# Nine elementwise steps of a gated delta rule and of a three-branch sum, issued on VectorE instead of GpSimd

## The chip, the cores and the metric

One core of a Trainium2 chip runs the whole program. It has TensorE (PE, with its weight loads as PEld), VectorE (DVE), ScalarE (ACT) and GpSimd (POOL), each with its own instruction queue that is worked off in order, and SyncE (SP), which here only issues DMAs. The engines wait for each other by semaphores. The metric is device time in microseconds: 1144.95 us, the median of three runs (1139.37, 1144.95, 1147.62).

## The reference

Two transformer blocks for 256 tokens of width 1024. The first block projects the tokens once and gives them to three branches (forgetting attention, a gated delta rule, stick-breaking attention). Their outputs are gated and summed; a memory attention and a feed-forward network follow, and then the second block. What the change touches is the decay of the delta rule and the gated sum:

```
qc, kc, vc, bc = chunks of 64 tokens of q * dk**-0.5, k, v, beta
gc    = cumsum(g within a chunk)
decay = exp(where(causal, gc[c] - gc[e], -inf))
kk    = kc @ kc.T
a_mat = where(strict, bc[c] * kk * decay, 0) + eye        # inverted further on
attn  = where(causal, (qc @ kc.T) * decay, 0)
...
mixed = g0 * (ya @ w_oa) + g1 * (yb @ w_ob) + g2 * (yc @ w_oc)
x     = x + mixed @ w_out
```

There are 4 heads of 128 and 4 chunks, so the 64x64 matrices of all heads and chunks fill a tile of 128 partitions x 512 elements (two chunks above each other, 8 pairs beside each other).

## The kernel before, in words

Nearly all time goes into products of activations with weights that stream from HBM, 512 KB at a time, in a fixed order. SP loads such a piece into one of three buffers (`raw`). ACT writes its rounded high part (`wh`, line 669), DVE the rest (`wl <- raw - wh`, line 670), and PE multiplies high by high, low by high and high by low (lines 508 to 558). A `raw` buffer is free for the next load when its `wl` is made. Up to four split pieces (`WEIGHTS = 4`) stand ready before PE.

Everything else (attention heads, the delta rule, norms, gates) is written as generators that yield where they would wait. While the program is built, a planner (`Pace` and `Stream`, lines 143 to 569) estimates when each engine is free and each operand is ready, and puts a generator's next step between the matmuls when its operands are expected. So the queues have one fixed order at run time, and it comes from the planner's costs: `70 + n / 0.96` ns for DVE, `150 + n * 2.1` ns for POOL (lines 206 to 209). Every instruction is issued through one helper, so the profile gives line 294 for all of them; they are told apart by their tiles.

The two places of the change:

- `Gdn.gates` (lines 1081 to 1150) makes the decay masks while PE is busy with the input projections. For each pair of heads (`j` = 0, 1) PE broadcasts the cumulated gates, DVE subtracts (`g<-pat,cols`), ACT makes `egB` and the exponentials `E` and `Eb`, and line 1136 multiplies `Eb` by `E`. Lines 1145 to 1148 then make `Em = E * m1l * eb`, `Eu = Eb * u1` and `E = E * uinc` of 128x512. Around them in DVE's queue are the `wl` of the weights and the convolution of the delta rule's inputs: one evacuation into `ypad`, two ACT steps and six `SCALAR_TENSOR_TENSOR g<-ypad,vec,g` of 128x256 for each pair of heads (lines 1152 to 1163).
- `mix` (lines 1729 to 1758) gates a branch's product with its output weights. The first branch writes the sum (`w_oc`), the second (`w_oa`, four pieces) multiplies and then adds into it at line 1743, the last (`w_ob`) does both on DVE.

Tiles: `g_893` holds `E` and `Eb`, `g_892` is `egB`, `g_1091` holds `Em` and `Eu`; `g_659` and `g_881` are convolved inputs; `sg` are gates, `a_280` and `a_286` the gated sum, `pmm` and `pat` tiles of PSUM.

Of the kernel before, what the change touches and what calls it, by code (L numbers as in the profile page):

```python
# [9 lines left out]
ALU = mybir.AluOpType  # L10
# [1017 lines left out]
class Gdn:  # L1028
# [52 lines left out]
    def gates(self):  # L1081

        K, nc = self.K, self.K.nc
        c, tl, v8 = self.c, self.tl, self.v8
        ident = K.C("ident")
        yield from K.room(pat=1)
        pc = K.pat()
        for t in range(2):
            nc.tensor.transpose(pc[:, t * 128:t * 128 + 68], c[0:68, t * P:t * P + P], ident[0:68, 0:68])
            nc.tensor.transpose(pc[:, 256 + t * 128:256 + t * 128 + 4], tl[64:68, t * P:t * P + P],  # L1090
                                ident[64:68, 64:68])
        K.drop(row=1)
        yield
        cols = K.p["tiny"].tile([P, 4, 4, 2], F32, tag="cols", bufs=1, name=K.nm("cols"))
        pcv = pc.rearrange("p (a t m) -> p a m t", a=2, t=2)
        lb, gc, be, tail = (cols[:, i] for i in range(4))
        nc.vector.tensor_copy(lb, pcv[:, 0, 32:36, :])
        nc.vector.tensor_copy(gc, pcv[:, 0, 64:68, :])
        nc.vector.tensor_copy(tail, pcv[:, 1, 0:4, :])
        K.drop(pat=1)  # L1100
        nc.vector.tensor_tensor(be, lb, gc, op=ALU.add)
        yield
        ecol = K.p["tiny"].tile([P, 4, 4, 2], F32, tag="ecol", bufs=1, name=K.nm("ecol"))
        nc.scalar.activation(ecol, cols, AF.Exp)
        self.eb, self.ebe, self.etail = ecol[:, 0], ecol[:, 2], ecol[:, 3]
        yield
        self.egB = K.g4()
        E, Eb = self.halves(K.g4())
        own = lambda a, c: a.rearrange("p (a m) -> p a m", a=4)[64 * c:64 * c + 64, :, 64 * c:64 * c + 64]
        for j in range(2):  # L1110
            hs, js = slice(2 * j, 2 * j + 2), slice(4 * j, 4 * j + 4)
            yield from K.room(pat=1)
            pg = K.pat()
            for h in range(2):
                K.mm(pg[:, h * T:h * T + T], K.sel("sel64", 2 * j + h), self.cg, True, True)
            yield
            for b in range(2):
                r = slice(64 * b, 64 * b + 64)
                gcb = gc[r, hs, :].rearrange("p h t -> p (h t)")[:, :, None].to_broadcast([64, 4, 64])
                nc.vector.tensor_tensor(E[r, js, :], own(pg, b), gcb, op=ALU.subtract)  # L1120
            nc.scalar.activation(self.egB[:, hs, :], pg.rearrange("p (a m) -> p a m", a=2), AF.Exp)
            K.drop(pat=1)
            yield
            nc.scalar.activation(E[:, js, :], E[:, js, :], AF.Abs)
            nc.scalar.activation(E[:, js, :], E[:, js, :], AF.Exp, scale=-1.0)
            yield
            yield from K.room(pat=1)
            pb = K.pat()
            for h in range(2):
                K.mm(pb[:, h * T:h * T + T], K.sel("sel0", 2 * j + h), self.cg, True, True)  # L1130
            yield
            for b in range(2):
                nc.scalar.activation(Eb[64 * b:64 * b + 64, js, :], own(pb, b), AF.Exp)
            K.drop(pat=1)
            yield
            nc.gpsimd.tensor_tensor(Eb[:, js, :], Eb[:, js, :], E[:, js, :], op=ALU.mult)
            yield
        K.drop(row=1)

        self.egl = K.p["tiny"].tile([P, 4, 4], F32, tag="egl", bufs=1, name=K.nm("egl"))  # L1140
        nc.vector.tensor_copy(self.egl, self.egB.rearrange("p h (n c) -> p h n c", n=4)[:, :, :, 63])
        cm = lambda name: K.C(name)[:, None, :].to_broadcast([P, 8, 64])
        ebb = self.eb.rearrange("p h t -> p (h t)")[:, :, None].to_broadcast([P, 8, 64])
        Em, Eu = self.halves(K.g4())
        nc.gpsimd.tensor_tensor(Em, E, cm("m1l"), op=ALU.mult)
        nc.gpsimd.tensor_tensor(Em, Em, ebb, op=ALU.mult)
        nc.gpsimd.tensor_tensor(Eu, Eb, cm("u1"), op=ALU.mult)
        nc.gpsimd.tensor_tensor(E, E, cm("uinc"), op=ALU.mult)
        self.Ec, self.Eb, self.Em, self.Eu = E, Eb, Em, Eu
        self.gated = True  # L1150
# [195 lines left out]
def model(K, aps):  # L1346
    nc = K.nc
# [9 lines left out]
    def job(loads, ncols, act, cb, **kw):  # L1357
        jobs.append(Job(loads, ncols, act, cb, **kw))
# [73 lines left out]
    def pair_of(*lz):  # L1432
        return lambda n: lz[n // 4]()[:, n % 4:n % 4 + 2, :]
# [295 lines left out]
    def mix(w, y, b, first, last):  # L1729
        dm = pair_of(*mixed)  # L1730
        left = [2, 2]

        def part(q, n):
            if last and mact.v is None:
                mact.v = K.new_act(8)
            dg, d = sgb[b][n // 4]()[:, n % 4:n % 4 + 2, :], dm(n)
            if first:
                K.tt(d, q, dg, ALU.mult)
            else:
                K.tt(dg, q, dg, ALU.mult)  # L1740
                if not last:
                    yield
                K.tt(d, d, dg, ALU.add, None if last else nc.gpsimd)
            if last:
                yield
                for e in range(2):
                    K.split_hi(mact.v, n + e, d[:, e, :])
                yield
                for e in range(2):
                    K.split_lo(mact.v, n + e, d[:, e, :])  # L1750
            left[n // 4] -= 1
            if left[n // 4] == 0:
                done.add(f"mix{w}{n // 4}")

        def one(c):
            job([(w, c, 4)], 256, y, lambda ps: st.spawn(part(ps[0], 2 * c)),
                ready=lambda: nc.ready(sgb[b][c // 2]()) if f"gate{b}{c // 2}" in done else None)
        return one
# [30 lines left out]
    def mem_k(n0, n, **kw):  # L1789
        fm("w_mkv", n0, n, m1act, m1rb, lambda t: mk()[:, 2 * n0 + t:2 * n0 + t + 2, :], f"mk{n0}", **kw)(0)  # L1790

    branch = {"m": lambda n: mem_k(n, 1), "x": lambda n: xa_kv(n), "g": gates(2), "q": jq, "k": jk, "v": jv, "c": mix("w_oc", yc, 2, True, False),
              "h": gates(0, "w_oc"), "a": mix("w_oa", ya, 0, False, False), "i": gates(1, "w_oa"),
              "b": mix("w_ob", yb, 1, False, True)}
    for c in BRANCH_ORDER.split():
# [394 lines left out]
```

## Time and profile before

| | us |
|---|---|
| median of three runs | 1144.95 |
| the profiled execution | 1144.86 |
| its span, first to last instruction | 1143.1 |
| PE busy | 1113.9 (97%) |
| DVE busy | 762.0 (67%) |
| ACT busy | 668.1 (58%) |
| POOL busy | 251.3 (22%) |

PE is the engine that the kernel is built around. A microsecond in which PE stands still lengthens the run if nothing behind it has room to take it up. Busy time of PE counts matmuls at whichever clock they ran, so a stretch at half the clock looks as busy as one at full clock; the granted clock of a stretch has to be read beside it. It was 0.993 of full speed over the whole span.

### The profile page before, as it was taken

The page shows a single profiled execution, that of the slowest core. Times are in us where ns is not written, and L with a number is a line of the kernel's source. Part 1 is how long each engine was busy: PE and PEld are TensorE (multiplying, and loading weights), DVE is VectorE, ACT ScalarE, POOL GpSimd, SP SyncE. Part 2 cuts the span into 40 slices and gives each one's busy share as a digit, 9 for nine tenths or more (in the row PEclk, how much of TensorE's full clock was granted, in tenths as well). Part 3 has the DMA queues.
Part 4 walks back from the last instruction along what each step waited for, and adds up shares of the span by engine and source line. Part 5 has one row for each costly group of instructions (what it writes and reads, how often), then busy time and mean ns, then how long its engine had stood idle before and what let it go on. Part 6 is the DMA issues. An engine that isn't in the chain of part 4 may idle for free.

```text
span 1143.1 us, 22340 instructions
## 1 busy us (share of the span) xinstructions
PE 1113.9 (97%) x9108; PEld 1063.6 (93%) x9108; DVE 762.0 (67%) x1016; ACT 668.1 (58%) x1084; POOL 251.3 (22%) x235
## 2 busy tenths in 40 slices
PE   8998999999999999999999999999999998999997
PEld 8997988999997999999999999998989998999986
DVE  5876785558786678888556555448876747555553
ACT  5556873476786666666546555546567557545442
POOL 0002121032032024334014333012102112533200
PEclk9998999999999999999999999999999999999999
DMA  7563633335565365555656655664444434656562
GB/s 243 167 212 129 192 98 112 110 111 185 166 207 163 93 195 177 184 183 177 213 182 204 203 194 186 203 205 158 163 149 147 160 86 138 205 188 204 189 207 100
DMA packets 56550, 193.96 MB, mean 170 GB/s; under 512 B 6400, under 2 KB 6528, under 8 KB 56448
## 3 DMA queue, kind: packets, MB, share of 16 engines
q1 hardware_dynamic: 56304, 192.54, 52.5%
q8 instruction: 71, 1.16, 0.4%
q14 instruction: 31, 0.25, 0.1%
q10 hardware_dynamic: 144, 0.01, 0.0%
HBM read 191.47 MB, written 1.05 MB: 168 GB/s over the span
## 4 chain that ended last, share of the span: by engine, by line
PE 67%; DVE 15%; ACT 7%; issue 5%; DMA 5%; POOL 0%; DVEq 0%; ACTq 0%; SPq 0%
PE pmm L294 57%; PE pat L294 10%; DVE wl L294 6%; DMA raw<-w_in 4%; ACT wh L294 3%; DVE a L294 3%; DVE g L294 2%; DVE s L294 2%; ACT s L294 2%; DVE sg L294 1%; DVE ypad L294 1%; ACT g L294 1%; DVE x L294 1%; ACT L294 1%; POOL s L294 0%
## 5 line engine op out<-in xcount | busy, mean ns | idle before, releaser
L294 DVE TENSOR_TENSOR wl<-raw,wh 128x1024 fp32r<-128x1024 f32 (+1 forms) x370 | 458.2, 1246 | 282.7 <-ACT wh L294 275.9
L294 PE MATMUL pmm<-a,wh 128*128 128x256 f32 x3792 | 492.0, 281 | 6.4 <-ACT wh L294 3.4
L294 ACT ACTIVATE wh<-raw 128x1024 fp32r<-128x1024 f32 (+1 forms) x370 | 373.3, 1019 | 173.8 <-DMA raw<-w_in 50.1
L294 PEld LDWEIGHTS pmm<-a,wh 128*128 128x128 f32 x3792 | 462.2, 189 | 12.6 <-ACT wh L294 5.1
L294 PE MATMUL pmm<-a,wl 128*128 128x256 f32 x1896 | 263.3, 281 | 6.4 <-DVE wl L294 6.2
L294 PEld LDWEIGHTS pmm<-a,wl 128*128 128x128 f32 x1896 | 238.6, 189 | 10.0 <-DVE wl L294 8.8
L294 PE MATMUL pmm<-g,wh 128*128 128x256 f32 x1088 | 138.1, 279 | 0.2
L294 PEld LDWEIGHTS pmm<-g,wh 128*128 128x128 f32 x1088 | 130.7, 188 | 0.9 <-DVE g L294 0.3
L294 POOL TENSOR_TENSOR sq<-sq,sq 128x512 f32<-128x512 f32 x30 | 43.0, 1435 | 336.7 <-ACT sq L294 335.2
L294 POOL TENSOR_TENSOR s<-s 128x256 f32<-128x256 f32 x66 | 73.0, 1107 | 172.5 <-ACT s L294 168.4
L294 ACT ACTIVATE s<-s 128x256 f32<-128x256 f32 (+4 forms) x117 | 55.7, 478 | 84.9 <-DVE s L294 69.3
L294 POOL TENSOR_TENSOR g<-s,g 128x256 fp32r<-128x256 f32 x66 | 64.4, 976 | 59.2 <-ACT g L294 59.2
L294 PE MATMUL pmm<-g,wl 128*128 128x256 f32 x544 | 74.6, 279 | 0.0
L294 PEld LDWEIGHTS pmm<-g,wl 128*128 128x128 f32 x544 | 67.8, 188 | 0.3 <-DVE wl L294 0.2
L294 ACT ACTIVATE g<-s 128x256 fp32r<-128x256 f32 x66 | 27.3, 413 | 57.1 <-POOL s L294 57.1
L294 POOL TENSOR_TENSOR s<-s,s 128x512 fp32r<-128x512 f32 (+1 forms) x25 | 31.5, 1267 | 94.3 <-ACT s L294 94.3
L294 DVE SCALAR_TENSOR_TENSOR s<-ypad,vec,s 128x256 f32<-128x256 f32 x88 | 45.3, 574 | 0.0
L294 PE MATMUL pmm<-wh,a 128*128 128x512 f32 x160 | 41.9, 399 | 0.3 <-DVE g L294 0.3
L294 DVE TENSOR_TENSOR s<-pmm,rb 128x512 f32<-128x512 f32 x44 | 30.2, 689 | 13.3 <-PE pmm L294 13.1
L294 ACT ACTIVATE a<-x,vec 128x256 fp32r<-128x256 f32 x54 | 24.8, 501 | 20.7 <-DVE x L294 20.7
L294 PEld LDWEIGHTS pmm<-wh,a 128*128 128x128 f32 x160 | 29.4, 188 | 6.6 <-DVE g L294 0.6
L294 DVE SCALAR_TENSOR_TENSOR a<-x,vec,a 128x256 fp32r<-128x256 f32 x56 | 32.9, 622 | 2.3 <-ACT a L294 2.3
(179 smaller groups left out, 929.3 us busy)
## 6 DMA issues: line engine op xcount, KB each, us to landing
raw<-ffn_w_up SPq DMA_DIRECT2D x82, 512.0 KB, 4.3
raw<-w_in SPq DMA_DIRECT2D x78, 512.0 KB, 4.1
raw<-ffn_w_down SPq DMA_DIRECT2D x42, 512.0 KB, 4.4
raw<-w_up SPq DMA_DIRECT2D x41, 512.0 KB, 4.2
raw<-w_down SPq DMA_DIRECT2D x20, 512.0 KB, 4.2
raw<-w_out SPq DMA_DIRECT2D x16, 512.0 KB, 4.1
raw<-xa_wkv SPq DMA_DIRECT2D x16, 512.0 KB, 3.9
raw<-w_mkv SPq DMA_DIRECT2D x8, 512.0 KB, 4.3
```

The lines of the kernel that those rows point to most:

```text
L294: return fn(*args, **kwargs)
```

## The change

Nine `tensor_tensor` of POOL become `tensor_tensor` of DVE: the two `Eb * E` of 128x256, the two steps of `Em` and the one of `Eu` (128x512), and the four additions of the second branch into the gated sum (128x512). `E * uinc` stays on POOL, as do the other uses of POOL (sums of squares, low parts in the head norms, gating in the feed-forward networks). No DMA, matmul or activation is added or removed.

```
@@ Gdn.gates
-            nc.gpsimd.tensor_tensor(Eb[:, js, :], Eb[:, js, :], E[:, js, :], op=ALU.mult)
+            nc.vector.tensor_tensor(Eb[:, js, :], Eb[:, js, :], E[:, js, :], op=ALU.mult)
...
-        nc.gpsimd.tensor_tensor(Em, E, cm("m1l"), op=ALU.mult)
-        nc.gpsimd.tensor_tensor(Em, Em, ebb, op=ALU.mult)
-        nc.gpsimd.tensor_tensor(Eu, Eb, cm("u1"), op=ALU.mult)
+        nc.vector.tensor_tensor(Em, E, cm("m1l"), op=ALU.mult)
+        nc.vector.tensor_tensor(Em, Em, ebb, op=ALU.mult)
+        nc.vector.tensor_tensor(Eu, Eb, cm("u1"), op=ALU.mult)
         nc.gpsimd.tensor_tensor(E, E, cm("uinc"), op=ALU.mult)
@@ mix
-                K.tt(d, d, dg, ALU.add, None if last else nc.gpsimd)
+                K.tt(d, d, dg, ALU.add)
```

Since the planner's costs differ for the two engines, some instructions also change their places. Before, DVE's queue in the decay masks, from the evacuation of one convolution to the weights behind it (`wl` are low parts of weight pieces; `ypad` and `g_659` belong to the convolution):

```order
L294 TENSOR_TENSOR ypad<-pmm_953,rb_418 128x2x256
L294 TENSOR_TENSOR wl_1022<-raw_912,wh_1021 128x1024
L294 TENSOR_TENSOR wl_1046<-raw_951,wh_1045 128x1024
L294 SCALAR_TENSOR_TENSOR g_659<-ypad,vec,g_659 128x256 x6
L294 TENSOR_TENSOR wl_1075<-raw_988,wh_1074 128x1024
L294 COPY egl_1089<-g_892 128x16
L294 TENSOR_TENSOR wl_1101<-raw_1025,wh_1100 128x1024
L294 TENSOR_TENSOR wl_1122<-raw_1049,wh_1121 128x1024
L294 TENSOR_TENSOR wl_1153<-raw_1078,wh_1152 128x1024
```

The same place of DVE's queue in the changed kernel, from the six steps of that convolution on (`g_1105` is now the tile of `Em` and `Eu`):

```order
L294 SCALAR_TENSOR_TENSOR g_659<-ypad,vec,g_659 128x256 x6
L294 TENSOR_TENSOR wl_1050<-raw_951,wh_1049 128x1024
L294 TENSOR_TENSOR wl_1073<-raw_988,wh_1072 128x1024
L294 TENSOR_TENSOR g_893<-g_893 128x256
L294 TENSOR_TENSOR wl_1094<-raw_1019,wh_1093 128x1024
L294 COPY egl_1103<-g_892 128x16
L294 TENSOR_TENSOR g_1105<-g_893,con 128x512
L294 TENSOR_TENSOR g_1105<-g_1105,ecol_847 128x512
L294 TENSOR_TENSOR g_1105<-g_893,con 128x512
L294 TENSOR_TENSOR wl_1122<-raw_1053,wh_1121 128x1024
L294 TENSOR_TENSOR wl_1153<-raw_1076,wh_1152 128x1024
```

The pieces 1022, 1046, 1075 and 1101 of before are 1016, 1050, 1073 and 1094 now. The six steps of the convolution have moved ahead of the second of them, one `Eb * E` stands before the fourth, and the three steps of `Em` and `Eu` before `wl_1122`. The other `Eb * E` (`j` = 0) stands further ahead, behind `wl_948`. PE has the same matmuls; two pairs of small ones (`pat<-cg,selr`) stand a few places later.

ACT's queue at the same place, before (`g_892` is `egB`, which in both kernels waits for the subtraction on DVE that reads the same `pat`):

```order
L294 ACTIVATE wh_984<-raw_870 128x1024
L294 ACTIVATE g_892<-pat_998 128x512
L294 ACTIVATE wh_1021<-raw_912 128x1024
L294 ACTIVATE g_659<-ypad,vec 128x256 x2
L294 ACTIVATE g_893<-g_893 128x256 x2
L294 ACTIVATE wh_1045<-raw_951 128x1024
```

And in the changed kernel:

```order
L294 ACTIVATE wh_984<-raw_870 128x1024
L294 ACTIVATE wh_1015<-raw_912 128x1024
L294 ACTIVATE g_659<-ypad,vec 128x256 x2
L294 ACTIVATE g_892<-pat_1027 128x512
L294 ACTIVATE wh_1049<-raw_951 128x1024
L294 ACTIVATE g_893<-g_893 128x256 x2
```

The high part of the next weight piece and the start of the convolution now come ahead of `egB`. In the gated sum only DVE's queue changes. This is its stretch before (`g_2647` is the delta rule's output in its norm):

```order
L294 TENSOR_TENSOR wl_3010<-raw_2873,wh_3009 128x1024
L294 TENSOR_TENSOR sg_2612<-pmm_3015,sg_2612 128x512
L294 TENSOR_TENSOR wl_3056<-raw_2901,wh_3055 128x1024
L294 SCALAR_TENSOR_TENSOR g_2647<-g_2647,vec,s_430_2978 128x512
L294 TENSOR_TENSOR sg_2867<-pmm_3061,sg_2867 128x512
L294 TENSOR_TENSOR wl_3096<-raw_2967,wh_3095 128x1024
L294 TENSOR_TENSOR wl_3130<-raw_3013,wh_3129 128x1024
L294 TENSOR_TENSOR sg_2867<-pmm_3101,sg_2867 128x512
```

And in the changed kernel:

```order
L294 TENSOR_TENSOR wl_3010<-raw_2873,wh_3009 128x1024
L294 TENSOR_TENSOR a_280_1991<-a_280_1991,sg_2612 128x512
L294 TENSOR_TENSOR sg_2612<-pmm_3015,sg_2612 128x512
L294 TENSOR_TENSOR wl_3056<-raw_2901,wh_3055 128x1024
L294 SCALAR_TENSOR_TENSOR g_2647<-g_2647,vec,s_430_2978 128x512
L294 TENSOR_TENSOR sg_2867<-pmm_3061,sg_2867 128x512
L294 TENSOR_TENSOR wl_3095<-raw_2967,wh_3094 128x1024
L294 TENSOR_TENSOR a_280_1991<-a_280_1991,sg_2612 128x512
L294 TENSOR_TENSOR wl_3130<-raw_3013,wh_3129 128x1024
L294 TENSOR_TENSOR a_286_2029<-a_286_2029,sg_2867 128x512
L294 TENSOR_TENSOR sg_2867<-pmm_3100,sg_2867 128x512
```

Three of the four additions stand here between weights and products, the fourth one weight piece further on; all else keeps its order.

## Rows read from the trace of the kernel before

**Rows 1.** The page, part 1: busy us (share of the span) x instructions.

```profile
PE 1113.9 (97%) x9108; PEld 1063.6 (93%) x9108; DVE 762.0 (67%) x1016; ACT 668.1 (58%) x1084; POOL 251.3 (22%) x235
```

**Rows 2.** Waits of PE over the whole span: us in total, times, longest.

```profile
PE pmm L294 <- DVE wl L294: 6.2, 6, 3.9
...
PE pmm L294 <- ACT wh L294: 3.4, 5, 1.4
```

**Rows 3.** Timeline, 68 to 105 us: start, us, engine, tiles, [idle before <- releaser].

```profile
72.55 2.94 DVE L294 SCALAR_TENSOR_TENSOR g<-ypad,vec,g 128x256 f32<-128x256 f32 x6
...
73.81 1.00 POOL L294 TENSOR_TENSOR g<-g 128x256 f32<-128x256 f32 x1 [72.33 <-DVE g L294]
...
84.17 1.23 DVE L294 TENSOR_TENSOR wl<-raw,wh 128x1024 fp32r<-128x1024 f32 x1 [2.02 <-ACT wh L294]
...
84.87 1.12 POOL L294 TENSOR_TENSOR g<-g 128x256 f32<-128x256 f32 x1 [10.06 <-ACT g L294]
85.31 6.82 DVE L294 SCALAR_TENSOR_TENSOR g<-ypad,vec,g 128x256 f32<-128x256 f32 x6
...
87.37 2.05 PE L294 MATMUL pmm<-a,wh 128*128 128x256 f32 x16
...
88.59 2.86 POOL L294 TENSOR_TENSOR g<-g,con 128x512 f32<-128x512 f32 x2
...
92.05 1.21 DVE L294 TENSOR_TENSOR wl<-raw,wh 128x1024 fp32r<-128x1024 f32 x1
...
93.32 2.07 PE L294 MATMUL pmm<-a,wl 128*128 128x256 f32 x8 [3.90 <-DVE wl L294]
...
95.19 3.56 PE L294 MATMUL pmm<-a,wh 128*128 128x256 f32 x16
...
98.59 1.07 PE L294 MATMUL pmm<-a,wl 128*128 128x256 f32 x8
...
99.50 1.98 PE L294 MATMUL pmm<-a,wh 128*128 128x256 f32 x16
...
103.37 2.06 DVE L294 SCALAR_TENSOR_TENSOR g<-ypad,vec,g 128x256 f32<-128x256 f32 x5
```

**Rows 4.** Windows: us, busy (x) of PE, PEld, DVE, ACT, POOL, granted clock, DMA, GB/s.

```profile
89.40:93.30 3.90, 0.02 (x1) 0.00 (x0) 3.90 (x6) 0.79 (x1) 2.05 (x2) 0.80 0.00 0
93.30:95.10 1.80, 1.78 (x8) 1.78 (x9) 1.80 (x3) 0.00 (x0) 0.00 (x0) 0.50 0.38 107
95.10:98.50 3.40, 3.40 (x18) 3.40 (x17) 1.04 (x2) 1.06 (x1) 0.00 (x0) 0.50 0.69 242
```

**Rows 5.** Timeline, 250 to 300 us.

```profile
262.13 1.78 DVE L294 SCALAR_TENSOR_TENSOR g<-g,vec,s 128x512 f32<-128x512 f32 x1
...
264.44 3.43 DVE L294 TENSOR_TENSOR wl<-raw,wh 128x1024 fp32r<-128x1024 f32 x2
...
265.70 1.19 PE L294 MATMUL pmm<-a,wl 128*128 128x256 f32 x8 [1.05 <-DVE wl L294]
...
268.39 0.73 DVE L294 SCALAR_TENSOR_TENSOR g<-g,vec,s 128x512 f32<-128x512 f32 x1
...
269.05 2.32 DVE L294 TENSOR_TENSOR wl<-raw,wh 128x1024 fp32r<-128x1024 f32 x1
...
271.43 0.98 PEld L294 LDWEIGHTS pmm<-a,wl 128*128 128x128 f32 x8 [0.20 <-DVE wl L294]
```

**Rows 6.** Tile `sg`, 250 to 300 us: durations min/median/max, first and last start.

```profile
L294 POOL TENSOR_TENSOR a<-a,sg x4: 1295/1966/2287, 253.8 to 268.5; 128x512 f32<-128x512 f32 x4
```

**Rows 7.** Groups by form of DVE over the whole span: busy us, mean ns.

```profile
L294 DVE TENSOR_TENSOR a<-a,sg 128x512 f32<-128x512 f32 x4 | 2.8, 692 | 0.1
L294 DVE TENSOR_TENSOR g<-g,g 128x256 fp32r<-128x256 f32 x4 | 1.5, 420 | 0.0
```

**Rows 8.** Tile `raw`, 60 to 105 us: durations, and from a load's issue to landing.

```profile
L294 ACT ACTIVATE wh<-raw x14: 1042/1060/1064, 59.9 to 102.9; 128x1024 fp32r<-128x1024 f32 x14
...
DMA to landing us min/median/max: 3.5/4.3/6.8
```

## The prediction, made before the changed kernel ran

> **What bounds the kernel now.** I read the page's shares first. PE is busy for 97% of the span, DVE for 67%, POOL for 22% [rows 1]. So PE sets the time, and a change on DVE and POOL counts only where PE stands still because of them, or runs at its half clock because it stood still. The second view is therefore PE's list of waits: the largest group is PE waiting for low parts of weights (`wl`) from DVE, 6.2 us in six waits, and one of them alone lasts 3.9 us [rows 2]. The timeline shows where that one lies: PE stops behind the matmuls that begin at 87.37 and starts again at 93.32, when the `wl` that DVE began at 92.05 is there [rows 3]. That is inside the change's first place.
>
> Why was that `wl` late? In front of it stand six convolution steps that took 6.82 us, from 85.31 on. Five of the same steps at 103.37 took 2.06 us, or 0.41 each, so six should take 2.47; 4.35 us are too much [rows 3]. In the same time POOL worked through five multiplications of the decay masks, the first from 84.87, the last two until 91.45 [rows 3]. The group at 72.55, with one POOL multiplication beside it at 73.81, took 2.94, 0.47 too much [rows 3]. I read from this that a DVE step with two inputs in SBUF and a POOL step with two inputs in SBUF hold each other up: 4.35 us for five POOL steps, 0.87 for each. The six steps run in order and DVE is busy for the whole of 89.4 to 93.3, while the DMA engines do nothing: with `wl` late no load buffer is free, so it is not the supply of weights that is short [rows 4].
>
> The stop has an aftermath. The granted clock, 0.80 over the stop itself, is 0.50 of full speed, the level of 1.2 GHz, from 93.3 to 98.5 [rows 4]. Eight matmuls take 2.07 us at 93.32 and 1.07 at 98.59, sixteen take 3.56 at 95.19 and 1.98 at 99.50 [rows 3].
>
> The second place looks the same on a smaller scale. While POOL makes its four additions (1.30 to 2.29 us each) [rows 6], a DVE step that takes 0.73 at 268.39 takes 1.78 at 262.13, two `wl` take 3.43 and one takes 2.32 [rows 5], where one alone is 1.21 [rows 3]. PE waits for 1.05 us at 265.70, and its weight load for 0.20 at 271.43 [rows 5].
>
> **The change, part by part.** *Decay masks, what goes.* The five POOL steps of before become one (`E * uinc`), and the one at 73.81 goes too. The six convolution steps lose up to 4.35 us.
>
> *Decay masks, what comes onto DVE.* Two steps of 128x256 at 0.42 each, and three of 128x512 at 0.69 each, the prices of such steps with both inputs in SBUF [rows 7]: 2.91 us. Two of them read constants or columns repeated over the tile, which no row of DVE with both inputs in SBUF shows; I take the same price, since the bounds around it (0.41 for the convolution steps, 0.73 for the longest undisturbed step of 128x512 [rows 3, 5]) do not leave much else.
>
> *Does PE still stop?* I follow the three low parts behind the convolution. The first (`wl_1075` before, `wl_1073` now) was ready at 92.05 + 1.21 = 93.26. Ahead of it DVE gains 4.35 and gets one `Eb * E`, 0.42: 89.3 at the latest. The convolution now stands in front of the low part that waited 2.02 us for ACT at 84.17 [rows 3], and can fill that wait: 87.3 at best. PE needs it when the sixteen matmuls begun at 87.37 are issued. Eight take 0.91 from start to start (98.59 to 99.50), so that is at 89.2. So the wait is between 0.1 and nothing. The next (`wl_1094`) comes after the other `Eb * E`: 0.42 + 1.21 later, at 88.9 to 90.9, and PE needs it 24 matmuls later, at 91.9. Then come `Em`, `Em`, `Eu`, 2.07 us, and `wl_1122`, 1.21: 92.2 to 94.2. If the `E * uinc` left on POOL holds one of them up by 0.87, 93.1 to 95.1. PE needs it at 94.7. So at worst PE waits there for 0.4 us; I take none. ACT's share: the convolution no longer stands behind `egB`, which only brings it forward. The moved pairs of small matmuls are the same matmuls, and cost nothing as long as PE's queue is full.
>
> *The weights behind.* `raw` for `wl_1122` is free when `wl_1050` is made, one `wl` ahead of 87.3 to 89.3, so at 86.1 to 88.1. With 4.3 us to land and 1.06 for the high part [rows 8] it is ready at 91.5 to 93.5; PE needs it at 92.8. A load that took 6.8 [rows 8] would make it up to 96.0: this is the thin place, and a rival below.
>
> *Worth of the first place:* the stop of 3.90, and the half clock behind it, (2.07 - 1.07) + (3.56 - 1.98) = 2.58. Together **6.5 us**.
>
> *The four additions.* On DVE 4 x 0.69 = 2.8 us come [rows 7]; what falls away is 1.78 - 0.73 = 1.05, 3.43 - 2 x 1.21 = 1.0 and 2.32 - 1.21 = 1.1, so 3.2 [rows 3, 5]. The first addition stands well ahead of the `wl` for which PE waits at 265.70, the second behind it. That `wl` moves forward by the 1.05 of the step at 262.13, which is just the length of PE's wait. I take 1.05 + 0.20, less some 0.05 for the tie: **1.2 us**.
>
> *Sum.* 6.5 + 1.2 = 7.7 us. The profiled execution took 1144.86, so 1137.2. It stands 0.1 below the median of the three runs, which is nothing against their scatter of 8 us. I expect the 7.7 to reach the end: the order of PE's queue behind both places is unchanged, PE works for nearly all of the span, and every load and every step behind it is started by something that moves forward with it.
>
> **The rivals.** *A shorter wait in the same place.* The late load: a `raw` that needs 6.8 us instead of 4.3 makes the high part up to 96.0 instead of the 92.8 at which PE wants it, and the last POOL step makes `wl_1122` late by 0.4. For it speaks that three buffers leave little room and that DVE still has 2.9 us more to do there; against it, that the loads at the slow end were issued in a burst after the stop. If PE stops for half of that, 1.8 us, and the clock falls again for 2.58, the gain is 7.7 - 4.4 = 3.3: 1141.6.
>
> *DVE itself is what is short (the other side).* If the six steps at 85.31 were slow for a reason of their own, taking POOL away frees nothing, and the nine steps come on top in DVE's queue, in front of weights for which PE already waits. They would cost 2.91 + 2.77 = 5.7 us of PE's time: 1150.5. This decides from the point at which the steps shorten by less than what is added, so if they still take more than 6.82 - 2.91 = 3.9 us. For it speaks that DVE is busy in every moment of the stop [rows 4]. Against it: the same steps take 0.41 with POOL idle and 0.49 with one POOL step beside them [rows 3], and the same pattern shows in three other kinds of DVE steps in the second place [rows 5]. The Trainium skill says something for this rival, in Perfetto Trace Analysis, section Optimizing Scalar/DVE Operations: where DVE is saturated, giving work to ScalarE or even GpSimd may pay, which here would be the way back. The same sentence limits itself, since the two engines share a read port, and the stretched steps show that the limit weighs more here [rows 3, 5].
>
> *More than the sum.* With DVE ahead, PE's other waits shrink too: the remaining 6.2 - 3.9 - 1.05 = 1.25 us for `wl` and 3.4 for `wh` [rows 2]. Then 7.7 + 4.65 = 12.4: 1132.5. Most of these waits lie far from the change, so this is unlikely in full.
>
> *Given back later.* PE arrives earlier at a stretch whose pace ACT sets, and waits there. Time: 1144.9. Against it, ACT's work in such a stretch is started by PE's results.
>
> **How the numbers follow.** The forecast has 0.57, with its own range of 1134 to 1140 from the runs' scatter and the ties above. The shorter wait has 0.18, more than the sum 0.12, given back later 0.07, DVE short 0.06. The predicted time is 1137.2. The range that leaves out 2 in 10 reaches from 1131, which takes in most of the larger gain, to 1143, which takes in the shorter wait with a little scatter; what is given back and the slower case stay outside. A measurement of this kernel tells about 1% (11.4 us) from no change. Faster by that means below 1133.5: the larger gain, and a little scatter of the forecast, 0.18. Slower by that means above 1156.4, which not even the slower rival reaches by itself: 0.04. Within 1%: 0.78.
>
> **What would show it.** In the changed profile the six convolution steps near 82 to 86 us should take 2.5 to 3 us, no `wl` near 85 to 95 more than 1.3 except one beside `E * uinc`, PE should have no wait above 0.5 us between 76 and 100, and the granted clock should stay at full speed there. Near 260 the step of 1.78 and the `wl` should be at 0.7 and 1.2, except one beside the head norm's POOL step. PE's 6.2 us of waits for `wl` should fall to about 1. I am wrong if the steps stay long with POOL idle, if PE waits for `wh` or `wl` in the first place at another piece, or if the span moves by much less than PE's idle time and cold time together.

## The result, and the profile after

In the same comparison the changed kernel took 1136.8 us (median of 20 runs, 1131.63 to 1144.68) and the kernel before 1141.8 us (median of 20, 1138.65 to 1150.6). The ratio is 0.994, with a 95% interval of 0.9921 to 0.9958: faster by 0.6% (0.4 to 0.8% by the interval, so some 5 to 9 us; the medians lie 5.0 apart), within the 1% that the prediction called no change. The profiled execution took 1137.06 us with a span of 1134.9, against 1144.86 and 1143.1 before.

The page of the changed kernel, part 1, and PE's waits over the whole span (us in total, times, longest), to be laid beside [rows 1, 2]:

```profile
PE 1107.0 (98%) x9108; PEld 1056.3 (93%) x9108; DVE 760.1 (67%) x1025; ACT 670.0 (59%) x1084; POOL 237.0 (21%) x226
```

```profile
PE pmm L294 <- ACT wh L294: 4.2, 6, 1.8
...
PE pat L294 <- POOL s L294: 2.9, 4, 1.3
PE pmm L294 <- DVE wl L294: 2.2, 3, 1.2
```

Waits for `wl` fell from 6.2 to 2.2 us. Those for `wh` rose by 0.8, those for `s` from POOL by 0.5 (2.4 before). DVE has nine instructions more and 1.9 us less busy time, since its other steps are shorter by more than the nine cost.

The timeline of the changed kernel over the first place, the answer to [rows 3]:

```profile
73.47 2.46 DVE L294 SCALAR_TENSOR_TENSOR g<-ypad,vec,g 128x256 f32<-128x256 f32 x6
...
76.71 0.97 PE L294 MATMUL pmm<-wh,a 128*128 128x512 f32 x3 [0.51 <-DVE g L294]
...
81.79 2.46 DVE L294 SCALAR_TENSOR_TENSOR g<-ypad,vec,g 128x256 f32<-128x256 f32 x6
...
88.07 2.00 PE L294 MATMUL pmm<-a,wh 128*128 128x256 f32 x16
...
88.90 0.68 DVE L294 TENSOR_TENSOR g<-g,con 128x512 f32<-128x512 f32 x1
...
89.73 1.74 POOL L294 TENSOR_TENSOR g<-g,con 128x512 f32<-128x512 f32 x1 [88.25 <-DVE g L294]
89.91 1.07 PE L294 MATMUL pmm<-a,wl 128*128 128x256 f32 x8
90.23 1.78 DVE L294 TENSOR_TENSOR g<-g,con 128x512 f32<-128x512 f32 x1
```

Both groups of six convolution steps take 2.46 us (2.94 and 6.82 before). The eight matmuls at 89.91 are the ones that began at 93.32 before, after a stop of 3.90 us; they follow the sixteen at 88.07 without a gap. The one long DVE step left is the multiplication for `Eu`, 1.78 us beside POOL's `E * uinc`.

Windows of the changed kernel (columns as in [rows 4]):

```profile
89.40:93.30 3.90, 3.90 (x36) 3.90 (x36) 3.87 (x5) 1.93 (x2) 1.74 (x1) 1.00 0.65 225
93.30:95.10 1.80, 1.80 (x18) 1.80 (x17) 1.77 (x3) 1.13 (x2) 0.00 (x0) 1.00 0.42 116
95.10:98.50 3.40, 3.40 (x32) 3.40 (x31) 3.40 (x8) 2.14 (x4) 0.00 (x0) 1.00 0.85 284
106.00:113.00 7.00, 5.45 (x25) 4.53 (x25) 4.37 (x5) 6.87 (x11) 2.51 (x2) 0.76 0.22 71
```

The three stretches that stood at a granted clock of 0.80, 0.50 and 0.50 are at 1.00, and in the first of them the DMA engines, which did nothing before, are busy for 0.65 of it. The fourth window is new: at 106 the clock falls, and the timeline of the changed kernel shows behind what:

```profile
106.52 0.50 PE L294 MATMUL pat<-s,onesr 128*128 128x512 f32 x1 [0.42 <-ACT s L294]
107.86 0.49 PE L294 MATMUL pat<-s,onesr 128*128 128x512 f32 x1 [0.84 <-POOL s L294]
108.65 1.92 PE L294 MATMUL pmm<-a,wh 128*128 128x256 f32 x8 [0.29 <-ACT wh L294]
```

The same matmuls in the kernel before (timeline):

```profile
112.19 0.50 PE L294 MATMUL pat<-s,onesr 128*128 128x512 f32 x1
...
113.54 0.49 PE L294 MATMUL pat<-s,onesr 128*128 128x512 f32 x1 [0.85 <-POOL s L294]
114.32 1.18 PE L294 MATMUL pmm<-a,wh 128*128 128x256 f32 x8 [0.29 <-ACT wh L294]
```

PE arrives earlier, waits 0.42 us for ACT where the kernel before shows no wait, and eight matmuls take 1.92 us, at the half clock, where they took 1.18.

The second place, in the timeline of the changed kernel, against [rows 5]:

```profile
258.08 0.74 DVE L294 SCALAR_TENSOR_TENSOR g<-g,vec,s 128x512 f32<-128x512 f32 x1
...
259.34 1.21 DVE L294 TENSOR_TENSOR wl<-raw,wh 128x1024 fp32r<-128x1024 f32 x1
...
260.61 1.20 PE L294 MATMUL pmm<-a,wl 128*128 128x256 f32 x8
...
261.08 1.21 DVE L294 TENSOR_TENSOR wl<-raw,wh 128x1024 fp32r<-128x1024 f32 x1
```

The step of 1.78 us is at 0.74, the two `wl` of 3.43 together at 1.21 each, and PE's wait of 1.05 is gone.

**Where the gain stands along the program.** For every kernel below I took the starts of the same five PE instructions and compared the four intervals with those of the kernel before. Each interval spans the same matmuls in each kernel of this table. M0 is the first pair `pat<-cg,selr` behind 64 us (65.84 before), M1 the first `pat<-a,a` (104.94), M2 the `wl` matmuls behind the head norms' `onesr` pair (116.71), M3 `pat<-onesr,s` with one column (257.02), M4 the first `pmm<-g,wh` behind it (277.88). Plus is a gain in us.

| kernel | mask steps on | additions on | queue order | M0-M1 | M1-M2 | M2-M3 | M3-M4 | sum |
|---|---|---|---|---|---|---|---|---|
| changed | DVE | DVE | new | 6.39 | -1.88 | -0.02 | 1.29 | 5.78 |
| e1, masks only | DVE | POOL | new | 7.19 | -2.92 | -0.08 | -0.25 | 3.94 |
| e2, additions only | POOL | DVE | old (masks) | -0.10 | 0.57 | -0.02 | 1.31 | 1.76 |
| e4, old order | DVE | DVE | old | 4.37 | -4.58 | -0.39 | 0.71 | 0.11 |
| e9, POOL late | POOL, later | POOL | old | 5.42 | -0.41 | 0.01 | -0.02 | 5.00 |
| e8, new order on POOL | POOL | POOL | new | 7.05 | 0.68 | -0.01 | -0.03 | 7.69 |
| e10, masks POOL, additions DVE | POOL | DVE | new | 6.14 | 1.00 | -0.02 | 1.30 | 8.42 |
| e3, POOL reads beside | DVE | DVE | new | 5.22 | -4.85 | -0.60 | 0.87 | 0.64 |
| e5, no POOL in the masks | DVE | DVE | new | 5.87 | 0.37 | -0.03 | 1.32 | 7.53 |

One execution each. Where two kernels have the same instructions, the last two columns agree within 0.05 us in most pairs and 0.6 at worst (e3), and M0-M1 within 0.9 (the changed kernel and e1, e8 and e10); M1-M2 takes up part of what M0-M1 shows. The gains that the ratios of whole runs below amount to, each known to 2 to 4 us, agree with these sums within 1.4 us, but for e4 and e3: their ratios (0.9967 and 0.996) amount to 3.8 and 4.6 us where the table has 0.11 and 0.64. No trace shows where that comes from, so what is said of e4 and e3 below rests on their traces alone. What follows behind M4 is told in the part on the prediction.

### The profile page after: what moved, and what is told of

Read it like the earlier page. It is cut to its first block, busy times and chain, and to the rows that moved or that the text cites. A ratio compares the mean times of both kernels' runs of the same rounds, so it can differ in the third digit from the quotient of the medians.

```text
span 1134.9 us, 22335 instructions
## 1 busy us (share of the span) xinstructions
PE 1107.0 (98%) x9108; PEld 1056.3 (93%) x9108; DVE 760.1 (67%) x1025; ACT 670.0 (59%) x1084; POOL 237.0 (21%) x226
## 3 DMA queue, kind: packets, MB, share of 16 engines
HBM read 191.47 MB, written 1.05 MB: 170 GB/s over the span
## 4 chain that ended last, share of the span: by engine, by line
PE 65%; DVE 16%; DMA 7%; ACT 6%; issue 5%; POOL 1%; DVEq 0%; ACTq 0%; SPq 0%; POOLq 0%
PE pmm L294 54%; PE pat L294 11%; DVE wl L294 7%; DMA raw<-w_in 3%; ACT wh L294 3%; DVE a L294 2%; DVE s L294 2%; DVE g L294 2%; DMA raw<-ffn_w_up 1%; DMA raw<-w_up 1%; ACT s L294 1%; DMA raw<-w_down 1%; DVE sg L294 1%; DVE ypad L294 1%; POOL s L294 1%
## 5 line engine op out<-in xcount | busy, mean ns | idle before, releaser
L294 PE MATMUL pmm<-a,wl 128*128 128x256 f32 x1896 | 260.6, 279 | 2.4 <-DVE wl L294 2.2
L294 PEld LDWEIGHTS pmm<-a,wl 128*128 128x128 f32 x1896 | 235.7, 188 | 5.9 <-DVE wl L294 4.5
```

The source lines that it names most:

```text
L294: return fn(*args, **kwargs)
```

## Experiments

**Each half of the change alone.** e1 leaves the four additions on POOL, e2 leaves the masks there.

```
e1:  K.tt(d, d, dg, ALU.add, None if last else nc.gpsimd)
e2:  nc.gpsimd.tensor_tensor(Eb[:, js, :], ...)   and the two of Em, the one of Eu on nc.gpsimd
```

> Only the five steps of the decay masks are on VectorE, the four additions stay on GpSimd. Theory A (a VectorE step and a GpSimd step that both read SBUF hold each other up, and the change takes the GpSimd steps away from there): the stop of 3.9 us near 89 us and the half clock behind it are gone, the waits of PE near 258 us (1.05 and 0.2 us) stay, so 5 to 5.5 us below before, ratio 0.9952 +- 0.002. Theory B (the gain comes from the new order of the queues): the same, since the order of this part is new here too. Theory C (the additions matter as much): a gain below 4 us.

> Only the four additions are on VectorE, the masks stay on GpSimd. Theory A: the stop near 89 us stays at 3.9 us with its half clock, the wait of 1.05 us near 265 us falls to 0.2 or less, 1.2 to 1.4 us below before: ratio 0.9988 +- 0.002, hardly told from 1. Theory C: 3 us or more.

e1 had a ratio to the kernel before of 0.9973 (0.9946 to 0.9999), e2 of 0.9982 (0.9948 to 1.0015). Neither tells much by its time; their traces do. In e2 the stop is whole, as its timeline shows:

```profile
86.61 6.80 DVE L294 SCALAR_TENSOR_TENSOR g<-ypad,vec,g 128x256 f32<-128x256 f32 x6
...
94.59 1.19 PE L294 MATMUL pmm<-a,wl 128*128 128x256 f32 x8 [3.96 <-DVE wl L294]
```

In e1 PE has no wait between 75 and 103 us at all; its sum is 3.94 us, where 5 to 5.5 were expected, since M1-M2 takes 2.92 back. The halves stand apart in the table: masks in M0-M1, additions in M3-M4, nothing between M2 and M3, and 3.94 and 1.76 make 5.70 where the whole change has 5.78. So the two places are independent, and the stretch M1-M2 belongs to the masks.

**Engine or order?** The change does two things to the masks: it moves steps to DVE, and it shifts the convolution and some weights in the queues, because the planner prices the engines differently. Three kernels fill the other corners. e4 runs all nine steps on DVE but is priced as if they were on POOL, which gives the queue order of before. e8 runs all nine on POOL but is priced as if on DVE, which gives the new order. e9 is the kernel before, order and engines, with POOL's last five mask steps held back by one small multiplication and nine fills of a buffer that is not yet in use.

```
e4:  pace.issue("pool", ...); return pace.vector.engine.tensor_tensor(...)     # nine steps
e8:  pace.issue("dve", ...);  return pace.gpsimd.engine.tensor_tensor(...)     # nine steps
e9:  if j == 1:
+        nc.gpsimd.tensor_tensor(poolw[...128x64], E[:, 7:8, :], E[:, 7:8, :], op=ALU.mult)
+        for _ in range(9): nc.gpsimd.memset(poolw[...128x512], 0.0)
     nc.gpsimd.tensor_tensor(Eb[:, js, :], Eb[:, js, :], E[:, js, :], op=ALU.mult)
```

> The queues in the order of the kernel before, to the instruction, with the nine steps issued on VectorE at the place where they were issued to GpSimd. Theory A: the six convolution steps take 2.5 us instead of 6.8, the stop near 89 us shrinks to below 0.5 us and the clock stays up; time within 1.5 us of the changed kernel, ratio to before 0.995. Theory B: the stop stays, ratio 1.0 or more (up to 5.7 us of added VectorE work).

> The nine steps are issued on POOL as in the kernel before, but every engine's other instructions stand in the order of the changed kernel. With the old order on DVE (the run before this one), before and the changed kernel, it makes four corners of a square: engine by order. If the gain comes from the engine (POOL off the port that DVE reads by), this kernel keeps the stretched convolution steps and loses the gain of the masks: landmark of ACT's first table load 101 to 104 us where the changed kernel has 98.3, ratio to the kernel before 0.997 to 1.0. If the gain comes from the order alone (the mask steps behind the low part for which PE waits, the convolution ahead of egB), it keeps most of it: landmark below 100, ratio 0.995 or lower. If both are needed, it lands between, and the sum of the two single effects falls short of the changed kernel's 5.7 us at the first table load.

> The kernel before, in its own order, with the second half's five POOL multiplications held back some 4 us by one small POOL multiplication and nine fills (fills left DVE's steps alone in the run before this). If the six convolution steps were long only because POOL worked beside them, they take 2.5 us here, the low part behind them is ready at about 89 where PE wants it at 89.4, and the gain at ACT's first table load is 4 to 7 us with nothing moved to DVE and no new order; POOL's steps then lengthen the low parts behind by up to 0.9 each, which may cost PE up to 1 us. If it is the place of the convolution in DVE's queue (ahead of the low part that waits 2 us) that counts, the gain stays below 2 us, as in the run with the old order and nine steps on DVE.

Ratios: e4 0.9967 (0.9937 to 0.9996), e8 0.9942 (0.9912 to 0.9972), e9 0.996 (0.9928 to 0.9993). The timeline of e4:

```profile
86.16 2.46 DVE L294 SCALAR_TENSOR_TENSOR g<-ypad,vec,g 128x256 f32<-128x256 f32 x6
...
94.40 1.19 PE L294 MATMUL pmm<-a,wl 128*128 128x256 f32 x8 [0.90 <-DVE wl L294]
...
98.66 1.06 ACT L294 ACTIVATE wh<-raw 128x1024 fp32r<-128x1024 f32 x1 [4.12 <-DMA raw<-w_in]
...
111.29 0.50 PE L294 MATMUL pat<-s,onesr 128*128 128x512 f32 x1 [3.30 <-ACT s L294]
```

With POOL idle the six steps are short, in the old order too, and of the stop 0.90 us is left, where less than 0.5 was expected. But now the mask steps stand ahead of the `wl` behind; these come late, load buffers come free late, ACT waits 4.12 us for a load, its table load for the silu steps starts only at 103.07, and PE waits 3.30 us for ACT. What M0-M1 gained, M1-M2 gives back.

The timeline of e9:

```profile
84.69 0.30 POOL L1137 TENSOR_TENSOR poolw<-g 128x64 f32<-128x64 f32 x1 [7.71 <-ACT g L294]
85.04 5.21 POOL L1139 MEMSET poolw<- 128x512 f32 x9
...
86.74 2.46 DVE L294 SCALAR_TENSOR_TENSOR g<-ypad,vec,g 128x256 f32<-128x256 f32 x6
...
89.54 2.05 PE L294 MATMUL pmm<-a,wh 128*128 128x256 f32 x16
...
91.43 1.10 PE L294 MATMUL pmm<-a,wl 128*128 128x256 f32 x8
```

Nothing was moved to DVE and no queue was reordered; the steps are short, the stop is gone, and 5 us stay. (At ACT's first table load e9 is 3.70 us ahead of the kernel before, a little less than the 4 to 7 expected; its M0 lies 1.33 later.) This is the plainest evidence for the cause: five POOL steps at the wrong moment made the stop.

The timeline of e8:

```profile
81.08 2.46 DVE L294 SCALAR_TENSOR_TENSOR g<-ypad,vec,g 128x256 f32<-128x256 f32 x6
...
85.77 1.12 POOL L580 TENSOR_TENSOR g<-g 128x256 f32<-128x256 f32 x1 [10.15 <-ACT g L294]
...
87.95 1.27 DVE L294 COPY egl<-g 128x16 f32<-128x16 f32 x1
...
88.97 1.07 PE L294 MATMUL pmm<-a,wl 128*128 128x256 f32 x8
...
89.47 1.92 DVE L294 TENSOR_TENSOR wl<-raw,wh 128x1024 fp32r<-128x1024 f32 x1 [0.25 <-ACT wh L294]
...
258.13 1.20 PE L294 MATMUL pmm<-a,wl 128*128 128x256 f32 x8 [1.05 <-DVE wl L294]
```

The mask steps are on POOL, and the gain of the first place is all there: the new order has finished the convolution at 83.5, before POOL begins at 85.77, and what POOL then stretches (a `wl` of 1.92 instead of 1.22, a copy of 1.27 instead of 0.17) has slack. At the second place the order has nothing of that sort, and PE's wait of 1.05 us is back.

**Each at its place.** e10 is e8 with the four additions on DVE: `K.tt(d, d, dg, ALU.add)`.

> The order of the changed kernel, the mask steps on POOL, the four additions on DVE. If the order alone makes the gain of the first place, as in the run with all nine on POOL, it is 6.5 to 7.6 us at the first table load; if the engine alone makes that of the second, 1.2 to 1.5 us come at 291 us. The ratio to the kernel before is then 0.991 to 0.994. If the additions need POOL idle beside them in the first place too, nothing comes at 291.

Ratio 0.9938 (0.9904 to 0.9972). In the table it has the largest sum, 8.42: the first place as e8, the second, 1.30, as the changed kernel. ACT's table load at 291 us, which the expectation named, is not a good mark for the second place: between ACT's loads at 252 and 291 us e10 gains only 0.17 on the kernel before, where PE's marks show 1.30. Its profiled execution took as long as 1141.5 us of span, for the most part because of stretches far behind (last part).

**POOL put back beside the new order.** e3 adds five POOL multiplications that read `E` and write the unused buffer; e3b adds one small multiplication and twelve fills, so that POOL works but does not read.

```
e3:   if j == 1:
+         for _ in range(5): nc.gpsimd.tensor_tensor(poolw[...], E, E, op=ALU.mult)
e3b:  if j == 1:
+         nc.gpsimd.tensor_tensor(poolw[...128x64], E[:, 7:8, :], E[:, 7:8, :], op=ALU.mult)
+         for _ in range(12): nc.gpsimd.memset(poolw[...], 0.0)
```

> The changed kernel with the same order of all queues, and five GpSimd multiplications of 128x512 added beside the VectorE stretch of the masks; they read E when ACT has made it and write into a buffer that nobody reads before its own load. Theory A: VectorE's weight steps and mask steps between 85 and 93 us are stretched by 0.9 us for each of the five, 4 to 5 us in all, against 1 to 3 us of room, so PE stops again for 1 to 4 us and falls to half clock; 2 to 6 us slower than the changed kernel, ratio to before 0.996 to 1.0. Theory B: nothing changes, ratio 0.994, no step of VectorE longer than in the changed kernel.

> The changed kernel with POOL busy beside the masks as in the run with five multiplications, but filling a buffer with zeros (twelve fills of 128x512 behind one small multiplication): POOL works and writes, and reads nothing. If DVE is held up by POOL's reading of SBUF, no DVE step there lasts longer than its own time by more than 0.3 us (convolution steps 0.41 each), PE does not wait, and the first table load stands at 98.3 plus or minus 1. If any POOL step holds DVE up, the steps beside the fills are stretched as in the run with the multiplications, and the landmark is 101 to 102.

e3: ratio 0.996 (0.9931 to 0.9989). Its timeline:

```profile
83.75 8.51 POOL L1128 TENSOR_TENSOR poolw<-g 128x512 f32<-128x512 f32 x5 [82.27 <-ACT g L294]
...
86.58 1.26 DVE L294 TENSOR_TENSOR g<-g 128x256 f32<-128x256 f32 x1
...
87.77 2.06 DVE L294 TENSOR_TENSOR wl<-raw,wh 128x1024 fp32r<-128x1024 f32 x1
```

That of e3b, which took 1141.0 us in its one run:

```profile
84.31 1.22 DVE L294 TENSOR_TENSOR wl<-raw,wh 128x1024 fp32r<-128x1024 f32 x1
84.37 1.31 POOL L1127 TENSOR_TENSOR poolw<-g 128x64 f32<-128x64 f32 x1 [82.89 <-ACT g L294]
...
85.74 6.96 POOL L1129 MEMSET poolw<- 128x512 f32 x12
...
87.28 0.42 DVE L294 TENSOR_TENSOR g<-g 128x256 f32<-128x256 f32 x1
...
89.12 0.68 DVE L294 TENSOR_TENSOR g<-g,con 128x512 f32<-128x512 f32 x1
```

Beside multiplications an `Eb * E` takes 1.26 us, beside fills 0.42. ACT's first table load stands at 98.58, as expected for fills. So it is POOL's reading that holds DVE up. The Trainium skill says so in SBUF — State Buffer, section Who interferes with whom: a DVE step with two inputs in SBUF collides with a GpSimd step that reads SBUF, not with one that only writes. The traces agree (0.42 and 0.68 us beside 6.96 us of fills). They also show the other direction: the small POOL multiplication takes 0.30 us in e9, with DVE idle, and 1.31 here, where it starts 0.06 behind a `wl` of 1.22 and ends 0.15 behind it. Nor does a DVE step need two inputs to be held up: the copy of 128x16, which reads one tile, takes 1.27 us in e8 and 0.20 beside the fills. e3 also shows that the new order is no cure when both engines have the masks' load: the `wl` are late, PE stops for 0.89 us at 95.69 and waits for ACT for 2.94 at 109.51, and M1-M2 gives 4.85 back.

**The step left on POOL.** e5 moves `E * uinc` to DVE too.

```
-        nc.gpsimd.tensor_tensor(E, E, cm("uinc"), op=ALU.mult)
+        nc.vector.tensor_tensor(E, E, cm("uinc"), op=ALU.mult)
```

> The changed kernel with the last multiplication of the masks, E times uinc, on DVE too, so that POOL does nothing in that stretch. If POOL's step held up the multiplication that makes Eu (1.78 us beside it), that one is back at 0.7 and the added step costs 0.69: DVE's work for the masks is shorter by about 0.4 us, the low part behind them comes as early or 0.4 earlier, and PE, which did not wait there, gains nothing: ratio to the kernel before 0.994 plus or minus 0.002, as the changed kernel. If the rival holds that DVE has no room left there, the low part comes later and PE waits 0.3 us or more in 88 to 95 us.

Ratio 0.9933 (0.9909 to 0.9957), by its time the same as the changed kernel. The `Eu` and `uinc` steps take 1.28 us together where the one took 1.78. The difference in the table, 5.87 + 0.37 against 6.39 - 1.88, is for the most part the half clock at 106 us, which did not come in e5, where PE had no wait at the first of those matmuls and 0.86 and 0.27 us at the next two. Its window:

```profile
105.00:113.00 8.00, 6.87 (x53) 6.16 (x53) 4.51 (x5) 7.83 (x14) 2.52 (x2) 1.00 0.22 59
```

But e9 waited 0.72, 0.85 and 0.29 there, longer than the changed kernel, and stayed at 1.00 as well. Why the clock falls in one and not in the other is open (last part).

**A break in ACT's run.** e7 is the changed kernel with a point between the four pairs of silu steps at which the planner may put other work of ACT; e11 is e5 and e12 is e10 with the same.

```
                 for b in range(2):
                     nc.scalar.activation(lz()..., lz()..., AF.Silu)
+                yield
```

> The changed kernel with a break between the eight silu steps of the convolutions in ACT's queue, so that high parts of weights and column sums can slip in between. Where the changed kernel gives back part of its gain, PE waits 0.42, 0.84 and 0.29 us at 106 to 109 us behind a run of ACT steps, and the clock falls to its half: about 1.55 us of waits and 1.8 us of half clock. If ACT's run is what paces that stretch, the waits and the half clock go and the landmark at 146 us stands 1 to 3 us earlier, ratio 0.991 to 0.993. If the waits come from POOL's step in the head norm instead, or the changed order costs as much elsewhere (more table loads, later weights), nothing is gained: ratio 0.994 or higher.

> The changed kernel with both edits that came out a little ahead of it: E times uinc on DVE, and a break between the silu steps. If their gains add, ratio 0.991 to 0.9925; if, as the landmarks behind 545 us suggest, what is gained ahead of it is no longer seen there, 0.993 to 0.995.

> What the runs so far point to, in one kernel: the order that the changed kernel has, the mask steps back on POOL behind the convolution, the four additions on DVE, and a break between the silu steps. If the parts add, PE's markers show about 7 us gained in the first place and the ACT-paced stretch behind it, some 2 more from the break and 1.3 from the additions, and the ratio to the kernel before is 0.989 to 0.992, below the changed kernel's 0.994. If what is gained ahead is no longer there behind 545 us, as the landmarks of the run with the break alone suggest, it is 0.993 to 0.995.

Ratios: e7 0.993 (0.9904 to 0.9955), e11 0.9908 (0.9877 to 0.994), e12 0.9901 (0.9865 to 0.9938). PE waits there not at all in e7, for 0.8 us in e11 and for 0.2 in e12, and by ACT's table load at 150 us these three are, in this order, 7.45, 7.65 and 7.48 us ahead of the kernel before, where the changed kernel is 4.08 ahead. (Their PE order differs, so the marks of the table do not hold for them.) At 291 us it is 9.35, 9.52 and 7.76, against 5.48, and at 545 us 5.04, 7.28 and 5.09, against 4.05: of a lead of some 3.5 us over the changed kernel at 150 us, 1.0 is left in e7 and e12, and 3.2 in e11. e11 and e12 have the lowest ratios of all, but their intervals overlap with that of the changed kernel, and they were not compared with it directly. That they beat it is likely, and not shown.

## Why the prediction was right, and where it was not

- **What stopped PE: right, and shown.** Short convolution steps go with POOL not reading beside them, in the old order (e4, e9) and in the new (changed, e8), on either engine; the stop goes with them, but for 0.90 us in e4.
- **Why it goes away: the wrong part of the change got the credit.** The prediction's step was that five POOL steps become one, and therefore the convolution loses 4.35 us; the new place of the convolution entered only as filling a wait. The runs show that the place is enough. With the order alone (e8) the first two intervals gain 7.73 us together, with the engine alone (e4) they lose 0.21, with both they gain 4.51, or 6.24 where the clock does not fall (e5). On DVE the mask steps may even cost some 1 to 1.5 us here, since they stand ahead of the `wl` that free load buffers (6.24 against 7.73 and 7.14 in e8 and e10); with one execution each, and 0.59 between e8 and e10, which have the same instructions there, this is not shown, and by their ratios (0.9933 against 0.9942 and 0.9938) the kernels do not differ.
- **Worth of the first place:** 6.39 measured in M0-M1, 6.5 forecast.
- **The nine steps on DVE:** 0.42, 0.68 and 0.69 as forecast. The one beside `E * uinc` was held up by 1.78 - 0.69 = 1.09 us, not 0.87, still without a wait of PE. The longest in 76 to 100 us is the 0.51 at 76.71, on the forecast's bound.
- **"I expect the 7.7 to reach the end": the step that failed.** 1.88 us are given back in M1-M2, in the way of the last rival, which had a chance of 0.07. ACT sets the pace there: from its first table load to M2 it is 12.75 to 12.78 us in each of the seven kernels of this PE order in which the clock did not fall (before, e2, e3b, e5, e8, e9, e10). In the changed kernel PE is 5.96 us earlier at M1 and ACT's table load only 5.68; so some 0.3 of the 1.88 is PE's wait for ACT. The other 1.6 is the half clock that came with it: from table load to M2 it is 14.35 us. The argument against the rival, that ACT's work there is started by PE's results, is wrong: ACT's silu run starts behind a `wh`, that behind a load, that behind a `wl` of DVE. In e4 this chain is 4.12 us long at one place. In the changed kernel the load is the one behind the first of these two `wl`:

```profile
91.93 2.35 DVE L294 TENSOR_TENSOR wl<-raw,wh 128x1024 fp32r<-128x1024 f32 x2
...
97.20 1.06 ACT L294 ACTIVATE wh<-raw 128x1024 fp32r<-128x1024 f32 x1 [1.25 <-DMA raw<-w_in]
...
98.28 1.28 ACT L294 ACT_TABLE_LOAD   x1
```

  Between ACT's table loads at 414 and 545 us another 1.4 are lost (132.04 us in the changed kernel, 130.62 before; PE waits there for 2.0 and 0.8 us). That this is the change's doing is not shown: every other profile lies between 131.14 and 133.11, e9 with the queues of before at 132.10.
- **The second place:** 1.29 measured (1.30 to 1.32 in e2, e5 and e10), 1.2 forecast. Here the engine is the cause: e8, in the same order, has none of it. But the order has a part too: in e4, where the second addition stands on DVE ahead of that `wl` and not behind it, the gain is 0.71, and PE still waits:

```profile
266.16 1.20 PE L294 MATMUL pmm<-a,wl 128*128 128x256 f32 x8 [0.65 <-DVE wl L294]
```

- **Waits for `wl`:** 2.2 us, where about 1 was forecast; waits for `wh` and `s` grew, since PE now arrives earlier at what others pace.
- **The number.** 1137.2 was forecast, 1136.8 measured, and that this is so close is luck. The forecast took 7.7 us from 1144.86; in the comparison the kernel before has a median of 1141.8, from which 7.7 would have left 1134.1, and the medians lie only 5.0 apart. A start 3.1 too high and a gain 2.7 too large cancel. The traces say the same of the gain: at 968 us the changed profile is only 3.8 us ahead. The profiled span is shorter by 8.2 because 4.05 more come between 968 and 1104 us, where the change touches nothing (last part).

## What to carry to other kernels

When an engine's steps are long beside another engine's, ask first whether the two can be kept apart in time: here a new place in the queue, or a later start, took away the whole stop, and moving the steps to the engine that was short gained no more than the new place alone. When a change also changes the order, build the two apart before crediting either. And follow a gain to the next stretch that another engine paces; what starts that engine is a chain of buffers, loads and weights, not only the engine that gained.

## What was not expected of the hardware

- **Two paces of matmuls at full clock.** Sixteen matmuls of 128x256 take 1.98 or 2.05 us, eight 1.07 or 1.10, both at a granted clock of 1.00, and one pace can hold for a hundred microseconds. The same stretch of the kernel before and of the changed one (timelines):

```profile
1000.11 2.05 PE L294 MATMUL pmm<-a,wh 128*128 128x256 f32 x16
```

```profile
1000.61 1.98 PE L294 MATMUL pmm<-a,wh 128*128 128x256 f32 x16
```

  From 968 to 1104 us 37 of the 38 groups of sixteen in the kernel before take 2.05 us and 37 of the 38 in the changed one 1.98: 136.44 us against 132.39. In e10 and e2 the stretch from 602 to 724 us has the slow pace (126.81 and 126.60 us, against 122.07 before). Every one of the profiles has stretches of either pace, whatever the order and the engine, so it is not tied to the change; at 3% of a stretch it is nearly as large as the whole gain. Its cause is open. It may be a good part of the scatter of the runs, which was not tested.
- **The half clock is not decided by the waits alone.** At 106 to 113 us it fell in the changed kernel behind waits of 0.42, 0.84 and 0.29 us, and not in e9 behind 0.72, 0.85 and 0.29. Of the eleven kernels with this order of PE, five wait 0.42 us or more in front of the first `pat<-s,onesr`; in four of them the clock fell (changed, e1, e3, e4: 0.42, 1.53, 2.94 and 3.30), and in e9 it did not. The matmuls just ahead of the wait had the slow pace in those four (2.05 us for sixteen) and the fast one in e9 (1.98). Whether the pace has to do with it was not tested.
- **A fill costs DVE nothing.** Nine fills of 128x512 took 5.21 us of POOL without lengthening a step of DVE, and served as a delay.
